# A two-block transformer step on one core: weight chunks multiplied in pairs at new buffer offsets, squares moved from POOL to ACT, first loads in another order

## The chip, the cores and the metric

The kernel runs on one core of one Trainium2 chip. The metric is the device time of one execution in microseconds (us). The profile is of one execution, and the times are medians of several runs.

## The reference, cut to what matters

256 positions with a width of 2048 pass through two transformer blocks in float32. Block 1: a banded attention (16 heads) beside a gated linear attention, an output projection, a feed-forward part with a causal convolution (5632 wide), and a gated side input, which this text calls the ple stage. Block 2: a sliding-window attention beside a stick-breaking attention, two gated branches, an output projection and a second feed-forward part. Nearly all arithmetic is in products with weight matrices that are read once:

```python
x = x + jnp.concatenate([y_a, y_g], axis=-1) @ w_out[i]
h = rms_norm(x, norm_ffn_w[i])
u = causal_depthwise_conv(h @ w_ffn_up[i], w_ffn_conv[i], b_ffn_conv[i])
u_gate, u_val = jnp.split(u, 2, axis=-1)
x = x + (jax.nn.gelu(u_gate) * u_val) @ w_ffn_down[i]
h = rms_norm(x, norm_ple_w[i])
x = x + jax.nn.sigmoid(h @ w_ple_gate[i]) * (p[i] @ w_ple_proj[i])
...
merged = jax.nn.sigmoid(ga) * ya + jax.nn.sigmoid(gb) * yb
x = x + merged @ w_out[layer]
x = x + swiglu(rmsnorm(x, norm_ffn_g[layer]), w_ffn_in[layer], w_ffn_down[layer])
```

Each norm needs the sum over the width of the squares of x.

## The kernel before

**Products.** Activations are held transposed (width on the 128 partitions, 256 positions along the row). A float32 product is made of fp32r products: each operand is the sum of a high part (its cast to fp32r, made by ACT) and a low part (the rest, made by DVE). An activation tile (`xa`, `g`, `m`, `pt`) holds high and low part side by side, 512 columns. A weight tile of 128x128 takes two matmuls: its high part against all 512 columns, its low part against the 256 high columns alone. Both accumulate in one PSUM bank, and the evacuation adds the bank's halves: ACT copies one half (`jb`, line 311), DVE adds the other (`jo`, by way of the helper in line 114).

**Chunks.** Weights come in chunks of 512 KB (128x1024: 4 tiles of the sum's index kk by 2 tiles of the output's index m, so 8 weight tiles). SP loads a chunk into one of 5 `raw` buffers; `split` (line 181) lets ACT write the high part (line 195) and DVE the low part (line 196) into one of 4 `hi` and one of 4 `lo` buffers. These are 1152 wide, and the chunk starts `off` elements into both: 48 (192 bytes), 80 for `w_out_2`, 72 for the ple stage's resident weights. `job_t` (line 236) makes one job, that is two output tiles, of several chunks, and takes two of four PSUM banks (`lin`). `overlap` (line 267) interleaves the first two jobs of a stage.

**Order.** Everything is put out in one hand-made order, and each engine runs its own part of it in that order. `run` (line 198) goes through the chunks: `open` (line 218) puts out loads and splits up to two chunks ahead (three in the ple stage), `multiply` (line 212) the matmuls, `step` (line 126) lets the generators of the evacuations, norms and attention heads each go on to their next `yield`, and `after` starts the evacuation of a job that has ended. `multiply` goes by runs of two tiles: two high matmuls, then the two low ones:

```python
for b in range(0, len(ch.tiles), RUN):        # RUN = 2
    for lo in range(2):
        for m, kk in ch.tiles[b:b + RUN]:
            ch.product(ch, m, kk, lo)
```

**The ple stage** (line 979) alternates a gate job of four chunks with one resident chunk of half the size (`pt`, 4 weight tiles), eight times. `ev_proj` (line 1009) takes the two output tiles of a resident chunk one after the other: in one step, for each, ACT's copy, DVE's sum, its product with the gate and its addition to x, then `sum_squares` (line 334): POOL squares x and POOL adds the square to `acc`. Two steps later, for each: ACT scales x, ACT and DVE make the next block's activation tile `g` from it, ACT squares it, POOL adds the square to `accb`.

**The start.** `start` (line 522) loads `mix_w` by ACT's queue, and puts out the loads of chunk 0 ahead of the rest: two halves of `x_in` and the second half of the weights on SP's queue, the first half of the weights on ACT's (`queues`). Nine matmuls of ones against ones follow, with nothing to compute.

Of the kernel before, what the change touches and what calls it, by code (L numbers as in the profile page):

```python
# [10 lines left out]
F32R = mybir.dt.float32r  # L11
# [6 lines left out]
P = 128  # L18
T = 256
D = 2048  # L20
KD = D // P
EPS = 1e-6
D_FF = 5632
KF = D_FF // P
# [26 lines left out]
RAW = 5  # L51
HL = 4
AHEAD = 2
RUN = 2

OFF = 48
OFF_OF = {"w_out_2": 80, None: 72}
LIN = 4


# [8 lines left out]
class Chunk:  # L69
# [6 lines left out]
    def __init__(self, dram, n, needs, mm, before=None, after=None, resident=None):  # L76
        self.dram, self.n, self.needs, self.mm = dram, n, needs, mm
        self.before, self.after, self.resident = before, after, resident
        self.pre_load = self.pre_split = None
        self.cuts, self.pack = 1, None  # L80
        self.ahead, self.queues = AHEAD, ()
        self.off, self.product, self.tiles = 0, None, None
        self.raw = self.hi = self.lo = None

    def of(self, part, n):
# [5 lines left out]
class Builder:  # L91
# [75 lines left out]
    def load_ahead(self, upto):  # L167

        while self.loaded < min(len(self.chunks), upto):
            ch = self.chunks[self.loaded]  # L170
            if ch.dram is not None:
                ch.raw = self.raw_p.tile([P, 1024], F32, tag="raw", name="raw")[:, :ch.n]
                for i in range(ch.cuts):
                    part = ch.of(i, ch.n)
                    if ch.pre_load:
                        ch.pre_load(i)
                    q = ch.queues[i] if i < len(ch.queues) else self.nc.sync
                    q.dma_start(ch.raw[:, part], ch.dram[:, part])
            self.loaded += 1

    def split(self, ch):
        hi = self.hl_p.tile([P, 1152], F32R, tag="hi", name="hi")[:, ch.off:]
        lo = self.hl_p.tile([P, 1152], F32R, tag="lo", name="lo")[:, ch.off:]
        ch.hi, ch.lo = hi[:, :2 * ch.n if ch.pack else ch.n], lo[:, :ch.n]
        raw = ch.resident() if ch.resident else ch.raw
        for i in range(ch.cuts):
            part = ch.of(i, ch.n)
            if ch.pre_split:
                ch.pre_split(i)
            r, hi, lo = raw[:, part], ch.hi[:, part], ch.lo[:, part]  # L190
            if ch.pack:
                r = r.rearrange("p (k c) -> p k c", c=ch.pack)
                both = ch.hi.rearrange("p (k s c) -> p k s c", s=2, c=ch.pack)
                hi, lo = both[:, :, 0], both[:, :, 1]
            self.nc.scalar.copy(hi, r)  # L195
            self.tt(lo, r, hi.bitcast(F32), ALU.subtract)

    def run(self):

        self.loaded = 0  # L200
        self.done = 0
        for i, ch in enumerate(self.chunks):
            self.open(i, ch.ahead)
            if ch.mm:
                ch.mm(ch)
            else:
                self.multiply(ch)
            self.step()
            if ch.after:
                ch.after()  # L210

    def multiply(self, ch):
        for b in range(0, len(ch.tiles), RUN):
            for lo in range(2):
                for m, kk in ch.tiles[b:b + RUN]:
                    ch.product(ch, m, kk, lo)

    def open(self, i, ahead):
# [14 lines left out]
        self.live_lin += 1  # L233
        return self.lin_p.tile([P, 512], F32, tag="lin", name="lin")

    def job_t(self, w, k0, kn, j, src, evac, before=None, resident=None, banks=None):

        ps = []
        for b in range(0, kn, 4):
            n = min(4, kn - b)

            def product(ch, m, kk, lo, b=b):
                k = b + kk
                if not ps:
                    ps.extend(banks() if banks else [self.lin_tile(), self.lin_tile()])
                at = kk * 256 + m * P
                self.nc.tensor.matmul(  # L250
                    ps[m][:, T:] if lo else ps[m], lhsT=(ch.lo if lo else ch.hi)[:, at:at + P],
                    rhs=src.tile[k][:, :T] if lo else src.tile[k], start=not lo and k == 0,
                    stop=bool(lo) and k == kn - 1, skip_group_check=True)
            after = None
            if b + n == kn:
                def after():
                    for m in range(2):
                        self.hot.append(evac(m, ps[m]))
            self.chunks.append(Chunk(
                None if resident else self.a[w][j, (k0 + b) // 4], n * 256,  # L260
                [(src, b + kk) for kk in range(n)], None, before=None if b else before,
                after=after, resident=resident))
            c = self.chunks[-1]
            c.off = OFF_OF.get(w, OFF)
            c.product, c.tiles = product, [(m, kk) for m in range(2) for kk in range(n)]

    def overlap(self, at, n):
# [204 lines left out]
    def block1(self):  # L472
        nc, a = self.nc, self.a
        h = Src(KD)
# [47 lines left out]
        def start():  # L522
            self.inv = None
            self.mix_w = s1.tile([P, KD], F32, tag="mix_w", name="mix_w")
            nc.scalar.dma_start(self.mix_w, a["mix_w"])
            self.load_ahead(1)
            nc.scalar.preload_act_table_set(LOG_SET)
            self.act_set = LOG_SET
            self.make_consts()

            ps = self.bank2(1)[:, 0, :P]
            for _ in range(9):
                nc.tensor.matmul(ps, lhsT=self.ones, rhs=self.ones, start=True, stop=True)
            self.wup = s1.tile([2 * RANK + 1, GH * DK], F32, tag="S", name="wup")
            self.lr = s1.tile([2 * RANK + 1, T], F32, tag="kt", name="lr")
            nc.gpsimd.memset(self.lr, 1.0)
# [23 lines left out]
            self.chunks[2 * i].pre_load = load_x(i)  # L560
            self.chunks[2 * i].pre_split = scale_x(i)
        self.chunks[0].cuts = 2
        self.chunks[0].queues = (nc.scalar,)
        self.chunks[0].tiles.sort(key=lambda t: t[1])
        for j in range(2):
            self.job_t("w_gq", 0, KD, j, h,
# [94 lines left out]
        for j in range(KD // 2):  # L661
            self.job_t("w_out", 0, KD, j, y,
                       self.ev_res(2 * j, h2, "norm_ffn_w", self.xa, "xa", lambda: acc2[0]),
                       before=open_x if j == 0 else None)
        self.overlap(at, 4)

    def put_y(self, y, k, x):
# [228 lines left out]
    def ffn(self, wu, wd, conv):  # L896
        nc, a = self.nc, self.a
        h = self.h_ffn
# [22 lines left out]
        for si, (f0, fn) in enumerate(segs):  # L921
            g = Src(fn)

            def ev_gate(j0):
                def ev(m, ps):
                    o = yield from conv_of(ps, j0 + m)
                    gt = self.ft.tile([P, T], F32, tag="gt", name="gt", bufs=4)
                    self.act(gt, o, AF.Gelu_apprx_tanh if conv else AF.Silu)
                    st[j0 + m] = gt
                return ev  # L930
# [9 lines left out]

            at = len(self.chunks)
            for j in range(f0, f0 + fn, 2):
                self.job_t(wu, 0, KD, j // 2, h, ev_gate(j))
                self.job_t(wu, 0, KD, (KF + j) // 2, h, ev_val(j))
            if si == 0:
                self.overlap(at, 4)
            final = si == len(segs) - 1
# [7 lines left out]
            for j in range(KD // 2):  # L955
                if not final:
                    ev = ev_down(2 * j)
                elif conv:
                    ev = self.ev_res(2 * j, out, "norm_ple_w", self.xa, "xa", lambda: acc[0])
                else:  # L960
                    ev = self.ev_final(2 * j)
                before = None
                if final and j == 0:
                    def before():
                        acc.append(self.new_acc())
                        self.acc_f = acc[0]
                        if conv:
                            self.open_ple()
                self.job_t(wd, f0, fn, j, g, ev, before=before)
            self.overlap(at, fn // 4)  # L970


# [6 lines left out]
    def ple(self):  # L979
# [29 lines left out]
        def ev_proj(k0):  # L1009
            def ev(m, ps):  # L1010
# [5 lines left out]
                gt = st.pop(k)  # L1016
                self.tt(t, t, gt, ALU.mult)
                self.tt(x, x, t, ALU.add)
                self.sum_squares(accs[0], x, k == 0)
                yield  # L1020
                yield

# [51 lines left out]
    def block2(self):  # L1074
# [123 lines left out]
            order += [("a", j), ("b", j)]  # L1198
        for kind, j in order:
            if kind == "a":  # L1200
                self.job_t("w2_ga", 0, KD, j, h, ev_ga(2 * j, ga))
                self.job_t("w_branch_a_2", 0, 8, j, ya, ev_ba(2 * j, ga))
            else:
                self.job_t("w2_gb", 0, KD, j, h, ev_ga(2 * j, gb))
                self.job_t("w_branch_b_2", 0, 8, j, yb, ev_bb(2 * j, gb),
                           before=close_att if j == 0 else None)
        h2 = Src(KD)
        self.h_ffn = h2
        acc = []
# [1 line left out]
        for j in range(KD // 2):  # L1211
            self.job_t("w_out_2", 0, KD, j, mg,
                       self.ev_res(2 * j, h2, "norm_ffn_g_2", self.xa, "xa", lambda: acc[0]),
                       before=(lambda: acc.append(self.new_acc())) if j == 0 else None)

        self.overlap(at, 4)
        self.close_mg = es2.close
# [218 lines left out]
```

## Time and profile before

| what | value |
|---|---|
| median of 3 runs | 2600.23 us (2600.16 to 2602.01) |
| profiled execution, its own time | 2600.7 us |
| its span, first to last instruction | 2599.0 us |
| mean granted TensorE clock | 0.998 |
| TensorE matmul busy | 2576.2 us, 99% of the span |
| DVE, ACT, POOL busy | 66%, 52%, 21% |

PE is TensorE's matmuls, PEld its weight loads, which run beside them. The duration of a matmul in the profile is from its start to its modelled end, and neighbours overlap; the rate is read from the starts of neighbouring matmuls. The profiled execution is 0.5 us over the median, and 1.7 us of its time lie outside the span.

### The profile page before, as it was taken

Reading aid. Unit: us, or ns where it says so; the run is one execution under the profiler, and the core shown is the slowest. Engines: PE = TensorE matmul, PEld = TensorE weight load, DVE = VectorE, ACT = ScalarE, POOL = GpSimd, SP = SyncE. Lnnn points to the kernel's source line nnn. Section 1 sums busy time; section 2 is a strip of 40 time slices with the busy share of each in tenths; the row PEclk is TensorE's granted clock in tenths of the full one; section 3 lists DMA queues with packets and bytes.
Section 4 is the critical chain, followed back from the end, with each engine's and each line's share of the span. In section 5 each row is a group of like instructions: output and inputs, shape, how many; then the busy total and the mean of one; then the engine's idle time right before and its main releaser. Section 6 shows DMA issues by size and latency. Waiting matters only on the chain.

```text
span 2599.0 us, 39038 instructions
## 1 busy us (share of the span) xinstructions
PE 2576.2 (99%) x14860; PEld 2239.3 (86%) x14860; DVE 1726.0 (66%) x2241; ACT 1351.2 (52%) x2018; POOL 556.8 (21%) x638
## 2 busy tenths in 40 slices
PE   9999999999999999999999999999999999999997
PEld 7888888888888888887878888888888888888886
DVE  7457677776677667778776766666665656555565
ACT  5545545564556445556555655554554444543543
POOL 5121232220122012346431111112311001100114
PEclk9999999999999999999999999999999999999999
DMA  7556575666666666654555456665666666666663
GB/s 245 157 163 191 168 234 186 195 190 193 187 191 190 193 187 190 223 175 149 167 152 156 148 166 199 192 189 191 189 193 189 193 191 190 192 190 190 191 192 124
DMA packets 133752, 480.36 MB, mean 185 GB/s; under 512 B 15067, under 2 KB 17371, under 8 KB 133436
## 3 DMA queue, kind: packets, MB, share of 16 engines
q1 hardware_dynamic: 131964, 474.19, 58.8%
q8 instruction: 116, 1.90, 0.3%
q0 software_dynamic: 736, 2.36, 0.3%
q10 hardware_dynamic: 864, 1.32, 0.1%
q14 instruction: 72, 0.59, 0.1%
HBM read 475.71 MB, written 2.10 MB: 184 GB/s over the span
## 4 chain that ended last, share of the span: by engine, by line
PE 93%; DVE 2%; POOL 1%; issue 1%; ACT 1%; DMA 0%; DVEq 0%; ACTq 0%; SPq 0%
PE lin L250 84%; PE lin L292 4%; PE lin L290 2%; DVE lo L114 1%; POOL cu L1002 1%; PE c L774 1%; DVE jo L114 1%; PE c L724 1%; PE c L761 0%; ACT hi L195 0%; PE c L250 0%; DMA x_in<-in_xT 0%; PE c L1253 0%; DVE x L114 0%; POOL x_in L506 0%
## 5 line engine op out<-in xcount | busy, mean ns | idle before, releaser
L114 DVE TENSOR_TENSOR lo<-raw,hi 128x1024 fp32r<-128x1024 f32 (+1 forms) x889 | 1133.2, 1286 | 616.6 <-ACT hi L195 614.2
L195 ACT CAST hi<-raw 128x1024 fp32r<-128x1024 f32 (+1 forms) x890 | 923.6, 1046 | 556.7 <-PE lin L250 501.1
L250 PE MATMUL lin<-xa,hi 128*128 128x512 f32 x3808 | 1186.6, 393 | 1.7 <-ACT hi L195 1.7
L250 PEld LDWEIGHTS lin<-xa,lo 128*128 128x128 f32 x3808 | 715.3, 188 | 162.6 <-DVE lo L114 6.2
L250 PE MATMUL lin<-g,hi 128*128 128x512 f32 x2592 | 807.4, 393 | 0.3 <-DVE jo L114 0.3
L250 PE MATMUL lin<-xa,lo 128*128 128x256 f32 x3808 | 753.7, 279 | 2.0 <-DVE lo L114 2.0
L250 PEld LDWEIGHTS lin<-xa,hi 128*128 128x128 f32 x3808 | 577.7, 188 | 4.5 <-issue 2.3
L250 PEld LDWEIGHTS lin<-g,lo 128*128 128x128 f32 x2592 | 486.7, 188 | 108.8 <-DVE lo L114 2.0
L250 PE MATMUL lin<-g,lo 128*128 128x256 f32 x2592 | 512.3, 279 | 0.8 <-DVE lo L114 0.8
L250 PEld LDWEIGHTS lin<-g,hi 128*128 128x128 f32 x2592 | 392.5, 188 | 3.7 <-issue 2.4
L910 POOL TENSOR_TENSOR cu<-jo,inv 128x256 f32<-128x256 f32 x176 | 133.2, 757 | 1083.3 <-DVE jo L114 1083.3
L311 ACT COPY jb<-lin 128x256 f32<-128x256 f32 x313 | 114.1, 372 | 193.1 <-PE lin L250 189.3
L114 DVE TENSOR_TENSOR jo<-lin,jb 128x256 f32<-128x256 f32 x297 | 122.3, 419 | 84.7 <-ACT jb L311 59.5
L329 ACT CAST g<-gt 128x256 fp32r<-128x256 f32 x88 | 35.8, 407 | 117.5 <-DVE gt L114 59.1
L117 DVE SCALAR_TENSOR_TENSOR co<-cu,vecs,co 128x255 f32<-128x255 f32 (+1 forms) x176 | 89.5, 529 | 3.1
L342 POOL TENSOR_TENSOR acc<-acc,sq 128x256 f32<-128x256 f32 x73 | 88.9, 1218 | 5.7
L340 POOL TENSOR_TENSOR sq<-x 128x256 f32<-128x256 f32 x73 | 55.2, 756 | 151.9 <-DVE x L114 151.7
L250 PE MATMUL lin<-m,hi 128*128 128x512 f32 x256 | 79.4, 392 | 0.0
L114 DVE TENSOR_TENSOR g<-gt,g 128x256 fp32r<-128x256 f32 x88 | 49.1, 558 | 25.0 <-ACT g L329 25.0
L114 POOL TENSOR_TENSOR gt<-gt,co 128x256 f32<-128x256 f32 x44 | 53.7, 1220 | 55.2 <-DVE co L117 55.2
L1155 POOL TENSOR_TENSOR u<-jo,inv 128x256 f32<-128x256 f32 x32 | 24.6, 772 | 176.9 <-DVE jo L114 176.9
L114 DVE TENSOR_TENSOR jo<-lin,x 128x256 f32<-128x256 f32 x128 | 53.1, 415 | 6.5 <-PE lin L250 6.5
(215 smaller groups left out, 1624.9 us busy)
## 6 DMA issues: line engine op xcount, KB each, us to landing
raw<-in_w_ffn_up SPq DMA_DIRECT2D x176, 512.0 KB, 4.1
raw<-in_w_ffn_down SPq DMA_DIRECT2D x176, 512.0 KB, 4.1
raw<-in_w_ffn_in SPq DMA_DIRECT2D x176, 512.0 KB, 3.8
raw<-in_w_out SPq DMA_DIRECT2D x64, 512.0 KB, 4.5
raw<-in_w_aq SPq DMA_DIRECT2D x32, 512.0 KB, 4.0
raw<-in_w_ple_gate SPq DMA_DIRECT2D x32, 512.0 KB, 4.0
raw<-in_w_ga SPq DMA_DIRECT2D x32, 512.0 KB, 3.7
raw<-in_w_gb SPq DMA_DIRECT2D x32, 512.0 KB, 3.7
```

Source lines behind the costliest of these rows:

```text
L114: (eng or self.nc.vector).tensor_tensor(out, a, b, op)
L117: self.nc.vector.scalar_tensor_tensor(out, in0=in0, scalar=scalar, in1=in1, op0=op0, op1=op1)
L195: self.nc.scalar.copy(hi, r)
L250: self.nc.tensor.matmul(ps[m][:, T:] if lo else ps[m], lhsT=(ch.lo if lo else ch.hi)[:, at:at + P], rhs=src.tile[k][:, :T] if lo else src. ...
L290: self.nc.tensor.matmul(ps[t][:, :wd], lhsT=xl, rhs=wt, start=k == 0, stop=False)
L292: self.nc.tensor.matmul(ps[t][:, :wd], lhsT=xh, rhs=wt, start=False, stop=bool(lo) and k == KD - 1)
L311: self.nc.scalar.copy(b[:n], ps[:n, T:])
L329: self.nc.scalar.copy(t[:, :T], x)
L340: g.tensor_tensor(sq, x, x, ALU.mult)
L342: g.tensor_tensor(acc, acc, sq, ALU.add)
L724: self.nc.tensor.matmul(ps[:, r, o], lhsT=q[r][rows[r], qs], rhs=k[rows[r], ks], start=True, stop=True, skip_group_check=True)
L910: nc.gpsimd.tensor_tensor(u, t, self.inv[:, :T], ALU.mult)
```

## The change

Chunks of jobs that are marked `paired` go two at a time where both have their operands: 16 high matmuls of both chunks, then their 16 low ones. Marked are `w_out`, both feed-forward parts, the branch and gate jobs of block 2 from the third pair on, and `w_out_2`: 32 + 264 + 72 + 32 + 264 = 664 chunks with 5,312 weight tiles. In them the high parts start 63 elements (252 bytes) into the buffer, the low parts 48 (192 bytes) as before; both are moved by the same 32 elements more for `w_out_2`. The others keep runs of two and their offsets. In `ev_proj`, the square for `acc` moves from POOL to ACT. Chunk 0's loads lose their place ahead of the others and their part on ACT's queue, and 11 matmuls of ones replace 9.

```diff
-RUN = 2
-OFF = 48
-OFF_OF = {"w_out_2": 80, None: 72}
+OFF = (48, 48)
+OFF_PAIRED = (63, 48)
+MORE_OFF = {"w_out_2": 32, None: 24}
...
-                    q = ch.queues[i] if i < len(ch.queues) else self.nc.sync
-                    q.dma_start(ch.raw[:, part], ch.dram[:, part])
+                    self.nc.sync.dma_start(ch.raw[:, part], ch.dram[:, part])
...
-        hi = self.hl_p.tile([P, 1152], F32R, tag="hi", name="hi")[:, ch.off:]
-        lo = self.hl_p.tile([P, 1152], F32R, tag="lo", name="lo")[:, ch.off:]
+        hi = self.hl_p.tile([P, 1152], F32R, tag="hi", name="hi")[:, ch.off[0]:]
+        lo = self.hl_p.tile([P, 1152], F32R, tag="lo", name="lo")[:, ch.off[1]:]
...
+        i = 0
+        while i < len(self.chunks):
+            some = self.chunks[i:i + 1]
+            self.open(i, some[0].ahead)
+            for ch in self.chunks[i + 1:i + 2]:
+                if (ch.paired and some[0].paired and not ch.before
+                        and all(src.ready[k] for src, k in ch.needs)):
+                    self.open(i + 1, AHEAD)
+                    some.append(ch)
+            if some[0].mm:
+                some[0].mm(some[0])
             else:
-                self.multiply(ch)
-            self.step()
-            if ch.after:
-                ch.after()
+                self.multiply([(ch, m, kk) for ch in some for m, kk in ch.tiles],
+                              16 if len(some) == 2 else 2)
+            for ch in some:
+                self.step()
+                if ch.after:
+                    ch.after()
+            i += len(some)
...
-            c.off = OFF_OF.get(w, OFF)
+            c.paired = paired
+            c.off = tuple(x + MORE_OFF.get(w, 0) for x in (OFF_PAIRED if paired else OFF))
...
-            self.load_ahead(1)
             nc.scalar.preload_act_table_set(LOG_SET)
...
-            for _ in range(9):
+            for _ in range(11):
                 nc.tensor.matmul(ps, lhsT=self.ones, rhs=self.ones, start=True, stop=True)
...
-        self.chunks[0].queues = (nc.scalar,)
...
                 self.tt(x, x, t, ALU.add)
-                self.sum_squares(accs[0], x, k == 0)
+                self.sum_squares(accs[0], x, k == 0, on_act=True)
                 yield
                 yield
```

## Rows read from the trace of the kernel before

**Rows 1.** The page's first part: engine, busy us, share of the span, instructions.

```profile
PE 2576.2 (99%) x14860; PEld 2239.3 (86%) x14860; DVE 1726.0 (66%) x2241; ACT 1351.2 (52%) x2018; POOL 556.8 (21%) x638
```

**Rows 2.** Windows, PE alone: window, length, busy (matmuls), clock, DMA share, GB/s.

```profile
420.00:1150.00 730.00, 730.00 (x4233) 1.00 0.63 193
1870.00:2480.00 610.00, 610.00 (x3538) 1.00 0.62 191
```

**Rows 3.** Timeline of PE: start, us, engine line operation, out<-in, count; feed-forward part.

```profile
2000.30 0.62 PE L250 MATMUL lin<-xa,hi 128*128 128x512 f32 x2
2000.76 0.39 PE L250 MATMUL lin<-xa,lo 128*128 128x256 f32 x2
2000.99 0.62 PE L250 MATMUL lin<-xa,hi 128*128 128x512 f32 x2
2001.44 0.40 PE L250 MATMUL lin<-xa,lo 128*128 128x256 f32 x2
2001.68 0.62 PE L250 MATMUL lin<-xa,hi 128*128 128x512 f32 x2
```

**Rows 4.** Timeline of PE: long run of 512-column matmuls, weights as moving operand.

```profile
107.25 0.39 PE L290 MATMUL lin<-hi,xa 128*128 128x512 f32 x1
...
109.06 1.07 PE L292 MATMUL lin<-lo,xa 128*128 128x512 f32 x4
```

**Rows 5.** Timeline of PE: long run of 256-column matmuls, weights as moving operand.

```profile
1258.65 0.28 PE L290 MATMUL lin<-hi,g 128*128 128x256 f32 x1
...
1260.57 1.12 PE L292 MATMUL lin<-lo,g 128*128 128x256 f32 x8
```

**Rows 6.** Timeline of PE: a resident chunk of the ple stage, one period earlier.

```profile
1203.05 0.62 PE L250 MATMUL c<-pt,hi 128*128 128x512 f32 x2
```

**Rows 7.** Timeline, all engines: one period of the ple stage; in brackets idle time and releaser.

```profile
1212.95 0.35 ACT L311 COPY jb<-c 128x256 f32<-128x256 f32 x1
...
1213.87 0.37 ACT L311 COPY jb<-c 128x256 f32<-128x256 f32 x1 [0.56 <-DVE jo L114]
...
1214.14 0.62 ACT L195 CAST hi<-w_ple 128x512 fp32r<-128x512 f32 x1
1214.33 0.42 DVE L114 TENSOR_TENSOR x<-x,jo 128x256 f32<-128x256 f32 x1
...
1214.84 0.61 POOL L340 TENSOR_TENSOR sq<-x 128x256 f32<-128x256 f32 x1 [2.24 <-DVE x L114]
...
1215.61 0.51 ACT L111 ACTIVATE x<-x,vecs 128x256 f32<-128x256 f32 x1
...
1215.76 0.86 DVE L114 TENSOR_TENSOR x<-x,jo 128x256 f32<-128x256 f32 x1
...
1216.64 0.62 PE L250 MATMUL c<-pt,hi 128*128 128x512 f32 x2
...
1217.73 0.51 ACT L111 ACTIVATE x<-x,vecs 128x256 f32<-128x256 f32 x1 [0.77 <-POOL sq L340]
...
1219.41 0.42 ACT L111 ACTIVATE sq<-x 128x256 f32<-128x256 f32 x1 [0.62 <-POOL acc L342]
...
1219.73 1.98 ACT L195 CAST hi<-raw 128x1024 fp32r<-128x1024 f32 x2
```

**Rows 8.** Timeline of the start: matmuls of ones, chunk 0's first load, cast and matmul.

```profile
1.05 4.21 PE L533 MATMUL c<-ones 128*128 128x128 f32 x18 [1.05 <-POOL ones L439]
...
1.24 0.45 ACTq L178 DMA_DIRECT2D raw<-in_w_gk  x1
...
6.28 0.62 ACT L195 CAST hi<-raw 128x512 fp32r<-128x512 f32 x1 [1.11 <-DMA raw<-in_w_gk]
...
6.95 1.22 PE L250 MATMUL lin<-xa,hi 128*128 128x512 f32 x2 [1.69 <-ACT hi L195]
```

**Rows 9.** Timeline of PE: the first norm's sum over the width.

```profile
34.56 0.67 PE L375 MATMUL c<-acc,ones 128*128 128x256 f32 x2 [0.73 <-DVE acc L114]
```

**Rows 10.** Timeline of DVE at the end: the last output tile.

```profile
2584.24 0.42 DVE L114 TENSOR_TENSOR jo<-lin,x 128x256 f32<-128x256 f32 x1 [0.51 <-PE lin L250]
```

More of the change, by code (lines that the diff above doesn't have):

```diff
@@ L80, in __init__ @@
         self.cuts, self.pack = 1, None
-        self.ahead, self.queues = AHEAD, ()
-        self.off, self.product, self.tiles = 0, None, None
+        self.ahead = AHEAD
+        self.off, self.product, self.tiles, self.paired = (0, 0), None, None, False
         self.raw = self.hi = self.lo = None
@@ L201, in run, with multiply @@
         self.done = 0
[L202 to L205, printed above, removed]
-            else:
-                self.multiply(ch)
-            self.step()
-            if ch.after:
-                ch.after()
-    def multiply(self, ch):
-        for b in range(0, len(ch.tiles), RUN):
+        i = 0
[9 more added lines that the diff above has]
+                some[0].mm(some[0])
+            else:
+                self.multiply([(ch, m, kk) for ch in some for m, kk in ch.tiles],
[5 more added lines that the diff above has]
+            i += len(some)
+    def multiply(self, tiles, run):
+        for b in range(0, len(tiles), run):
             for lo in range(2):
-                for m, kk in ch.tiles[b:b + RUN]:
+                for ch, m, kk in tiles[b:b + run]:
                     ch.product(ch, m, kk, lo)
@@ L234, in lin_tile, with job_t @@
         return self.lin_p.tile([P, 512], F32, tag="lin", name="lin")
-    def job_t(self, w, k0, kn, j, src, evac, before=None, resident=None, banks=None):
+    def job_t(self, w, k0, kn, j, src, evac, before=None, resident=None, banks=None,
+              paired=False):
         ps = []
@@ L663, in block1 @@
                        self.ev_res(2 * j, h2, "norm_ffn_w", self.xa, "xa", lambda: acc2[0]),
-                       before=open_x if j == 0 else None)
+                       before=open_x if j == 0 else None, paired=True)
         self.overlap(at, 4)
@@ L942, in ffn @@
             for j in range(f0, f0 + fn, 2):
-                self.job_t(wu, 0, KD, j // 2, h, ev_gate(j))
-                self.job_t(wu, 0, KD, (KF + j) // 2, h, ev_val(j))
+                self.job_t(wu, 0, KD, j // 2, h, ev_gate(j), paired=True)
+                self.job_t(wu, 0, KD, (KF + j) // 2, h, ev_val(j), paired=True)
             if si == 0:
@@ L968, in before @@
                             self.open_ple()
-                self.job_t(wd, f0, fn, j, g, ev, before=before)
+                self.job_t(wd, f0, fn, j, g, ev, before=before, paired=True)
             self.overlap(at, fn // 4)
@@ L1200, in block2 @@
             if kind == "a":
-                self.job_t("w2_ga", 0, KD, j, h, ev_ga(2 * j, ga))
-                self.job_t("w_branch_a_2", 0, 8, j, ya, ev_ba(2 * j, ga))
+                self.job_t("w2_ga", 0, KD, j, h, ev_ga(2 * j, ga), paired=j > 1)
+                self.job_t("w_branch_a_2", 0, 8, j, ya, ev_ba(2 * j, ga), paired=j > 1)
             else:
-                self.job_t("w2_gb", 0, KD, j, h, ev_ga(2 * j, gb))
+                self.job_t("w2_gb", 0, KD, j, h, ev_ga(2 * j, gb), paired=j > 1)
                 self.job_t("w_branch_b_2", 0, 8, j, yb, ev_bb(2 * j, gb),
-                           before=close_att if j == 0 else None)
+                           before=close_att if j == 0 else None, paired=j > 1)
         h2 = Src(KD)
@@ L1213, in block2 @@
                        self.ev_res(2 * j, h2, "norm_ffn_g_2", self.xa, "xa", lambda: acc[0]),
-                       before=(lambda: acc.append(self.new_acc())) if j == 0 else None)
+                       before=(lambda: acc.append(self.new_acc())) if j == 0 else None,
+                       paired=True)
         self.overlap(at, 4)
```

## The prediction, made before the run

> **What bounds the kernel now.** I read the page first. PE is busy for 99% of the span and no other engine for more than 66% [rows 1], so whatever does not lengthen or shorten PE's own stream costs nothing, and the stream's rate is the first question. The windows of the two feed-forward parts give it: 4,233 matmuls in 730.00 us, 3,538 in 610.00 [rows 2], that is 172.4 ns per matmul and 345 ns per weight tile (one high, one low matmul), with no idle time at the full clock. The timeline shows what the 345 ns are made of: from one group of four to the next 0.69 us, of which two high matmuls take 0.45 or 0.46 (225 to 230 ns each) and two low ones 0.23 or 0.24 (115 to 120 each) [rows 3]. The other place to read is the ple stage, where PE does wait. Its period, from one resident chunk to the next, is 1216.64 - 1203.05 = 13.59 us [rows 6, 7], while 4 gate chunks and a resident one are 36 weight tiles, or 36 x 0.345 = 12.42. So 1.17 us of each period are lost, and what sets it is the order of work on ACT and DVE: ACT casts the weights of a chunk only when PE already needs them.
>
> The sum is made against the profiled execution, 2600.7 us, which stands 0.5 over the median of the runs.
>
> **Part 1, pairs and offsets.** 664 chunks with 5,312 weight tiles change their order and the place of their high parts. No matmul is added or removed. In a pair 15 of 16 high matmuls follow a high one, and 15 of 16 low ones a low one, so a tile costs one interval in a long run of each sort. No row shows this kernel's weights in such a run, or at 252 bytes. The nearest rows are the runs with the operands exchanged: 8 matmuls of 512 columns in 109.06 - 107.25 = 1.81 us, 226 ns each [rows 4], and 16 of 256 columns in 1260.57 - 1258.65 = 1.92 us, 120 ns each [rows 5]. Against them stand this kernel's own intervals, 225 to 230 and 115 to 120. The low end is 225 + 115 = 340 ns, the high end 230 + 120 = 350; times 5,312 that is -26.6 to +26.6 us. I take 226 for the high one, as in the long run, and 119 for the low one, near the long run but a little down, because the low parts keep their offset and have been seen at 115. That is 345 ns, and a change of 0.
>
> [...]
>
> **Part 2, what a pair holds up.** A pair lasts 16 x 0.345 = 5.5 us and holds two of the four high and low buffers. The casts for the next pair can start once its predecessor's high run is over, and ACT has two of them per 5.5 us at 52% busy [rows 1]: cost 0, and if that cover failed, each late cast would show as a PE wait. Where two overlapped jobs end in one pair (10 stage heads), their banks are wanted at once. The first job's low parts end 0.92 us and more before the pair does, and its two outputs take four DVE sums of 0.42 us (the duration in [rows 10]), so I take 0; with a weight split in front of them it would be 1 us each, +10 at the most, the lower end being 0 too, as nothing is released earlier. At the very end of the kernel the first of the last two outputs is complete 4 low matmuls (0.46 us) before the last matmul, now 4 tiles (1.38). It loses 0.92; DVE idles 0.51 there today [rows 10] and takes that up: **+0.4 us**.
>
> **Part 3, squares on ACT.** This is the part that I expect to decide. Per period POOL loses two squares and ACT gains two of about 0.42 us. ACT also loses two waits for POOL, 0.77 and 0.62 [rows 7]. That looks like a gain. But ACT works in order, and the new square stands behind DVE's addition to x and ahead of the second tile's copy `jb` and of the next casts. Step by step from [rows 7]: the first copy starts at 1212.95, and x is complete at 1214.33 + 0.42 = 1214.75. ACT's square starts at 1214.84, where POOL's does now, and ends at 1215.26. Only then the second copy runs (now 1213.87); it needs the same 1.80 us to its x (1212.95 to 1214.75), so x is there at 1217.06, and the second square ends at about 1217.57. Now the cast of the resident weights starts, which stood at 1214.14: 3.4 us later. From there to the scaling of x 1.47 us stay (1214.14 to 1215.61): 1219.04. The first tile's three ACT operations take 1217.73 - 1215.61 - 0.77 = 1.35, the second's 1219.73 - 1217.73 - 0.62 = 1.38, and the next cast starts at 1221.77 instead of 1219.73: 2.0 us later per turn of the loop. ACT's next turn starts from that cast, so the loop grows by that, and PE, which already waits for it, waits 2.0 more: for the resident weights' cast about 1.5 (they are wanted at 1216.64 and would be ready at 1218.2), then the rest at the next gate chunk. There are seven whole turns between eight resident chunks: **7 x 2.0 = +14.0 us**. Low end: only the waits and the squares count, 0.84 - 1.39 = -0.55 per turn, -4.4 over eight. High end: the 3.4 us at the cast in full, +24. I take the worked-out chain.
>
> **Part 4, the start.** The first weights move to SP's queue, behind the first half of x, and each later SP load comes 0.45 us later (the duration of an issue) [rows 8]; ACT's queue loses one issue. Today the first cast waits 1.11 us for these weights, and the first matmul runs at 6.95 [rows 8]. Between 1.1 us earlier and 0.45 later; either way PE then waits 0.73 us for the first norm's sum [rows 9], which ends with the last load of x and its squares, not with PE. Cost 0; without that cover -1.1 to +0.45. Eighteen recorded matmuls of ones take 4.21 us; four more (two calls) take 0.9 and end at about 6.2, before 6.95: cost 0, hidden by the same wait for the cast.
>
> **Sum.** 0 + 0.4 + 14.0 + 0 = +14.4 us: 2615.1 for the profiled execution, **2614.6 us** as a median (2600.2 + 14.4).
>
> **Rivals.**
> - *The pairs pay more than the ple stage loses (faster).* The place is the 5,312 tiles, the price up to 5 ns each; it decides from 14.4 / 5,312 = 2.7 ns per tile on. For it: both levels are there in today's stream, and 340 ns would only make the better one permanent [rows 3]. Against it: both long runs sit near the upper level for the low ones [rows 4, 5]. At 340 ns: 2614.6 - 26.6 = 2588. Chance 0.22.
> - *The pairs cost.* Long runs lock into the upper level, or the 252 bytes hurt: at 346 ns 2620, at 350 ns 2641. For it: 120 ns in the long run [rows 5]. Chance 0.17.
> - *The squares help.* The generators' order leaves ACT other work to do, and only the waits for POOL go: -4.4 + 0.4 gives 2596. For it: the 0.77 and 0.62 us; DVE's addition to x takes 0.86 beside POOL's work against 0.42 [rows 7]. The Trainium skill (SBUF — State Buffer, section Who interferes with whom) says that a DVE instruction with two SBUF inputs contends with a GpSimd instruction that reads SBUF; the two additions agree with it. Against it: the copy, the square and the next copy come out of one generator after the other in one step. Chance 0.12.
> - *The pairs don't form* because operands are not marked ready in time: then part 1 is 0 for those chunks, and the time is the forecast's.
>
> **How the numbers follow.** The forecast, with 2602 to 2630, has 0.45, and 0.04 goes to causes not named. About 0.2% (5 us) is what a measurement of this kernel can tell from no change. Faster by more: most of the first rival (0.15), half of the third (0.06), 0.01 of the rest: 0.22. Within it: the parts of these two near the present time (0.07 and 0.06): 0.13. Slower: 0.65. The range reaches from 2592, which takes in the third rival and the upper half of the first, to 2632, which takes in the pairs' cost up to 348 ns.
>
> **What would show it.** The windows of the feed-forward parts give the tile: 345 ns if part 1 is right, 342 or less for the first rival, 347 or more for the second. In the ple stage the period between resident chunks should be near 15.6 us, ACT should wait for DVE's x ahead of each square, and PE should wait for the cast of `w_ple`. PE's wait for the first norm should be there still. I am wrong if the period stays at 13.6 or falls, or if the feed-forward windows move by more than 2.7 ns per tile.

## The result and the profile after

The changed kernel takes **2641.84 us** (median; 2640.4 to 2642.6), the kernel before beside it 2600.48: a ratio of 1.0157 [1.014, 1.0175], 41.4 us slower. Slower was forecast (2614.6), but the time lies outside the range (2592 to 2632). The profiled execution took 2641.56 us.

The page's first part, as [rows 1]:

```profile
PE 2607.0 (99%) x14864; PEld 2250.8 (85%) x14864; DVE 1678.4 (64%) x2241; ACT 1350.0 (51%) x2034; POOL 527.6 (20%) x622
```

PE is still at work all the time, with four matmuls more (of ones, at the start) and 30.8 us more of it. So the stream itself has become slower. Stage lengths, from the starts of their first matmuls in both traces:

| stage | before | after | difference |
|---|---|---|---|
| up to `w_out` | 320.2 | 319.9 | -0.3 |
| `w_out` | 100.0 | 101.1 | +1.1 |
| first feed-forward part | 729.1 | 743.2 | +14.1 |
| ple stage | 105.7 | 118.3 | +12.6 |
| block 2 to its branches' end | 511.5 | 509.6 | -1.9 |
| `w_out_2` | 99.5 | 101.2 | +1.7 |
| second feed-forward part | 718.0 | 731.1 | +13.1 |

Windows of PE in the two feed-forward parts, as [rows 2]:

```profile
420.00:1150.00 730.00, 730.00 (x4157) 1.00 0.60 190
...
1930.00:2480.00 550.00, 550.00 (x3134) 1.00 0.58 187
```

Two matmuls per weight tile: 2 x 730 / 4157 = 351.2 ns, and 351.0 in the second, where before had 345 [rows 2]. The clock is full and PE never idles. The timeline of PE there, as [rows 3]:

```profile
2000.54 3.89 PE L262 MATMUL lin<-xa,hi 128*128 128x512 f32 x16
2004.27 2.05 PE L262 MATMUL lin<-xa,lo 128*128 128x256 f32 x16
2006.15 3.89 PE L262 MATMUL lin<-xa,hi 128*128 128x512 f32 x16
```

Sixteen high matmuls take 3.73 us, 233 ns each; sixteen low ones 1.88 us, 118 each. The median intervals are these to the ns in 296 of the 332 pairs. The other 36 are those of block 2's branches. Timeline of PE where they end and `w_out_2` begins:

```profile
1786.69 3.79 PE L262 MATMUL lin<-xa,hi 128*128 128x512 f32 x16
1790.32 1.98 PE L262 MATMUL lin<-xa,lo 128*128 128x256 f32 x16
1792.14 3.90 PE L262 MATMUL lin<-m,hi 128*128 128x512 f32 x16
1795.88 2.05 PE L262 MATMUL lin<-m,lo 128*128 128x256 f32 x16
1797.77 3.89 PE L262 MATMUL lin<-m,hi 128*128 128x512 f32 x16
```

At the offsets of the feed-forward parts, the branch pairs run at 3.63 / 16 = 227 and 1.82 / 16 = 113 ns, 340 per tile, and from the first `m` on (weights 128 bytes further) it is 351. Below, the two are called the slow and the fast stream.

The ple stage: timeline of PE (first two lines: turns of the loop, as the 1216.64 of [rows 7]) and three waits that were shorter or not there before (none, 1.23 and 0.21 us). The first of the three stands at the norm ahead of the stage and is part of the +14.1:

```profile
1238.36 0.74 PE L262 MATMUL c<-pt,hi 128*128 128x512 f32 x2 [1.12 <-ACT hi L195]
...
1253.25 0.73 PE L262 MATMUL c<-pt,hi 128*128 128x512 f32 x2 [1.15 <-ACT hi L195]
```

```profile
1164.21 0.70 PE L388 MATMUL c<-acc,ones 128*128 128x256 f32 x2 [0.77 <-POOL acc L355]
...
1193.66 1.02 PE L262 MATMUL c<-pt,hi 128*128 128x512 f32 x2 [3.13 <-ACT hi L195]
...
1282.50 0.46 PE L303 MATMUL lin<-hi,g 128*128 128x256 f32 x1 [3.36 <-ACT hi L195]
```

A turn takes 14.89 us instead of 13.59. ACT's timeline shows why:

```profile
1248.29 0.36 ACT L324 COPY jb<-c 128x256 f32<-128x256 f32 x1
1250.12 0.42 ACT L112 ACTIVATE sq<-x 128x256 f32<-128x256 f32 x1 [1.48 <-DVE x L115]
1250.45 0.35 ACT L324 COPY jb<-c 128x256 f32<-128x256 f32 x1
1252.28 0.42 ACT L112 ACTIVATE sq<-x 128x256 f32<-128x256 f32 x1 [1.48 <-DVE x L115]
1252.60 0.60 ACT L195 CAST hi<-w_ple 128x512 fp32r<-128x512 f32 x1
```

Before each square ACT stands idle for 1.48 us until DVE has x. From the first copy to the cast of the resident weights it now takes 4.31 us, in [rows 7] 1.19.

The start, as [rows 8, 9]:

```profile
5.77 0.86 PE L262 MATMUL lin<-xa,hi 128*128 128x512 f32 x2
...
34.24 0.67 PE L388 MATMUL c<-acc,ones 128*128 128x256 f32 x2 [0.78 <-DVE acc L115]
```

The first matmul runs 1.2 us earlier; the wait for the first norm is there as before (0.78 and 0.73 us), and 0.3 us are left of it.

### The profile page after: what moved, and what is told of

The parts are those of the page before. It is cut to its first block, busy times and chain, and to the rows that moved or that the text cites. A ratio compares the mean times of both kernels' runs of the same rounds, so it can differ in the third digit from the quotient of the medians.

```text
span 2639.6 us, 39353 instructions
## 1 busy us (share of the span) xinstructions
PE 2607.0 (99%) x14864; PEld 2250.8 (85%) x14864; DVE 1678.4 (64%) x2241; ACT 1350.0 (51%) x2034; POOL 527.6 (20%) x622
## 4 chain that ended last, share of the span: by engine, by line
PE 93%; DVE 2%; ACT 2%; POOL 1%; issue 1%; DMA 0%; DVEq 0%; SPq 0%; ACTq 0%
PE lin L262 84%; PE lin L305 4%; PE lin L303 2%; ACT hi L195 1%; PE c L785 1%; DVE jo L115 1%; PE c L735 1%; POOL cu L1013 1%; DVE x L115 0%; PE c L262 0%; PE c L772 0%; DVE lo L115 0%; PE c L1265 0%; ACT sq L112 0%; DMA raw<-in_w_gk 0%
## 5 line engine op out<-in xcount | busy, mean ns | idle before, releaser
L115 DVE TENSOR_TENSOR lo<-raw,hi 128x1024 fp32r<-128x1024 f32 (+1 forms) x889 | 1099.7, 1271 | 676.2 <-issue 349.2
L262 PE MATMUL lin<-xa,hi 128*128 128x512 f32 x3808 | 982.9, 395 | 0.6 <-DVE xa L118 0.4
L262 PEld LDWEIGHTS lin<-xa,hi 128*128 128x128 f32 x3808 | 673.9, 188 | 121.3 <-issue 2.3
L262 PE MATMUL lin<-g,hi 128*128 128x512 f32 x2592 | 667.6, 394 | 0.3 <-DVE jo L115 0.3
L262 PEld LDWEIGHTS lin<-xa,lo 128*128 128x128 f32 x3808 | 530.7, 188 | 55.9 <-DVE lo L115 5.6
L262 PE MATMUL lin<-xa,lo 128*128 128x256 f32 x3808 | 544.1, 280 | 2.2 <-DVE lo L115 2.2
L262 PEld LDWEIGHTS lin<-g,hi 128*128 128x128 f32 x2592 | 458.1, 188 | 82.5 <-issue 2.4
L262 PEld LDWEIGHTS lin<-g,lo 128*128 128x128 f32 x2592 | 360.4, 188 | 35.0 <-DVE lo L115 0.7
L262 PE MATMUL lin<-g,lo 128*128 128x256 f32 x2592 | 368.5, 279 | 0.3 <-DVE lo L115 0.3
L112 ACT ACTIVATE co<-cu,vecs 128x256 f32<-128x256 f32 x88 | 52.9, 603 | 101.5 <-POOL cu L921 97.4
L115 DVE TENSOR_TENSOR jo<-lin,x 128x256 f32<-128x256 f32 x128 | 53.2, 416 | 30.9 <-PE lin L262 30.8
```

The costliest lines, as they stand in the source:

```text
L112: self.nc.scalar.activation(out, in_, func, **kw)
L115: (eng or self.nc.vector).tensor_tensor(out, a, b, op)
L262: self.nc.tensor.matmul(ps[m][:, T:] if lo else ps[m], lhsT=(ch.lo if lo else ch.hi)[:, at:at + P], rhs=src.tile[k][:, :T] if lo else src. ...
```

## The experiments

**Order or place, pairs or squares?** The first four runs take one part each: the changed kernel with runs of two in its pairs; with the high parts back at 192 bytes; the kernel before with the square on ACT alone; the changed kernel with both parts at 0 bytes.

```diff
# e1_run2
-                              16 if len(some) == 2 else 2)
+                              2)
# e2_off48
-OFF_PAIRED = (63, 48)
+OFF_PAIRED = (48, 48)
# e3_squares, on the kernel before
-                self.sum_squares(accs[0], x, k == 0)
+                self.sum_squares(accs[0], x, k == 0, on_act=True)
# e4_off0
-OFF_PAIRED = (63, 48)
+OFF_PAIRED = (0, 0)
```

> The changed kernel with pairs kept, high parts at 252 bytes, but runs of two again (two high, two low). Theory A (the long run of one sort costs the 6.2 ns per weight tile): feed-forward windows back at 345 ns per tile, time near 2641.8 - 33 = 2609. Theory B (the 252 bytes cost it): 351 ns stay, time near 2642. Theory C (both are needed): between, 347 to 349, some 2625.

> The changed kernel with runs of 16, but high and low parts of paired chunks both at 192 bytes. Theory A (long run): 351 ns per tile stay, 2642. Theory B (offset): 345 or less, near 2609. Theory C: between.

> The kernel before with the squares for acc on ACT and nothing else. My chain: the ple stage's loop grows by 1.3 to 2.0 us per turn, the stage by 10 to 14, the time is 2611 to 2615. The rival (only the waits for POOL go): 2596. A third view, that the stage was longer in the changed kernel because of the pairs ahead of it: 2600.

> The changed kernel with runs of 16 and both parts of paired chunks at the buffer's start (0 bytes), where the exchanged-operand runs of the kernel before stood at 226 and 120 ns. If those rows carry over: 346.7 ns per tile, near 2618. If the long run costs at any offset (theory A): 351 or more, 2642 or more. If offsets matter in steps of the address: any value, and the first two runs tell less than they seem to.

The kernel before took 2601.49 us beside them. e1: 2643.17, e2: 2614.33, e3: 2614.91, e4: 2632.09. These four, and e5 to e8, e10 to e14 and e17, are single runs; kernels that ran more often spread over 1 to 3 us. So the order of the run does nothing to the rate, the place of the high parts is the loss in the stream, and the square on ACT costs 13.4 us by itself: 12.5 in the ple stage, which is 118.2 us long, and 0.9 in block 2. The window of PE in e2's first feed-forward part, and its timeline:

```profile
425.00:1130.00 705.00, 705.00 (x4091) 1.00 0.59 194
```

```profile
2001.55 3.84 PE L262 MATMUL lin<-xa,hi 128*128 128x512 f32 x16
2005.23 1.98 PE L262 MATMUL lin<-xa,lo 128*128 128x256 f32 x16
2007.04 3.82 PE L262 MATMUL lin<-xa,hi 128*128 128x512 f32 x16
2010.70 2.05 PE L262 MATMUL lin<-xa,lo 128*128 128x256 f32 x16
```

That is 344.7 ns per tile, as before; the low runs take 1.81 and 1.88 us by turns, so quicker and slower pairs alternate (5.49 and 5.54 us).

**Which places are slow?** Six further offsets in the changed kernel, with the square back on POOL. In the table below, the changed kernel, e2 and e4 have it on ACT, which costs their time some 13 us but not their rates.

```diff
-OFF_PAIRED = (63, 48)
+OFF_PAIRED = (0, 48)     # e5; e6 (60, 48), e7 (49, 48), e10 (62, 48), e11 (48, 49), e12 (60, 60)
...
-                self.sum_squares(accs[0], x, k == 0, on_act=True)
+                self.sum_squares(accs[0], x, k == 0)
```

> The changed kernel with its squares back on POOL, runs of 16, high parts at 0 bytes and low parts at 192. If high and low parts take their intervals each from their own offset (high 226.7 ns as in the run with both at 0, low 113 to 118 as in the run with both at 192): 341 to 345 ns per tile in the feed-forward windows, 2580 to 2601. If what counts is that both parts have the same offset: above 345, over 2605.

> As the last, but high parts at 240 bytes, a whole number of 16-byte steps, 12 bytes short of the change's 252. Theory M (252 is costly because it is no whole number of 16-byte steps): 345 ns per tile or near it, 2596 to 2606. Theory D (what counts is the distance from the activation operand, and 252 is simply in a bad stretch): near 351 ns, 2628 to 2635.

> As the last, but high parts at 196 bytes, one word off the good 192. Theory M (no whole number of 16-byte steps costs): near 351 ns per tile, 2628 to 2635. Theory D (distance in a smooth stretch): near 345, 2596 to 2606.

> The changed kernel with squares on POOL, runs of 16, high parts at 248 bytes (a multiple of 8, not of 16), low parts at 192. Theory M (steps of 16 bytes decide): high intervals near 233 ns, 349 to 351 per tile, 2620 to 2635. If steps of 8 bytes are enough: high intervals 226 to 230, 344 to 346 per tile, 2596 to 2606.

> The same with high parts at the good 192 bytes and low parts at 196. Theory M for weights of either sort: low intervals rise by about as much as the high ones did (4 to 6 ns over 113 to 118), 349 to 352 per tile, 2620 to 2640. If it is only beside 512 columns that an odd place costs: 345 to 346, 2600 to 2606.

> The same with high and low parts both at 240 bytes, a multiple of 16. Theory M: 344 to 347 per tile, 2595 to 2612; the low intervals tell whether 113 or 118 ns go with the offset (113 in all runs, or 118 in all) or come and go within one kernel, as they did with both at 192.

The kernel before took 2600.2 to 2600.3 us beside them. The time per tile is twice the window by its matmuls (705 us from 425, 550 us from 1930); the intervals, high and low, are means from the start of a matmul to the next, from 425 to 1130 us.

| run | bytes, high and low | us | ns per tile, first and second part | high, low |
|---|---|---|---|---|
| after | 252, 192 | 2641.84 | 351.2, 351.0 | 233, 118 |
| e2 | 192, 192 | 2614.33 | 344.7, 345.2 | 229, 116 |
| e4 | 0, 0 | 2632.09 | 347.5, 348.0 | 228, 120 |
| e5 | 0, 192 | 2620.73 | 347.8, 348.3 | 231, 118 |
| e6 | 240, 192 | 2604.05 | 345.0, 345.6 | 227, 118 |
| e7 | 196, 192 | 2619.01 | 350.4, 345.3 | 233, 118 |
| e10 | 248, 192 | 2613.41 | 347.0, 346.9 | 233, 114 |
| e11 | 192, 196 | 2618.23 | 347.6, 347.6 | 229, 118 |
| e12 | 240, 240 | 2611.53 | 345.2, 348.1 | 228, 117 |

None of these is clearly under 345. High parts at multiples of 16 bytes (0, 192, 240) run at 227 to 231 ns, those at 196, 248 and 252 at 233; this fits a step of 16 bytes, but the changed kernel's own 36 fast pairs, 227 at 252 bytes, speak against the address alone. e7 shows the same: 350.4 in one stage and 345.3 in another at the same offsets, the low interval being 118 in one and 113 in the other.

**Squares without the wait, and the start.** The square stays on ACT, but two steps later, when x has long been there: in the kernel before (e8), and in the changed kernel with pairs never formed and the offsets of before (e9). The edit in e9; in e8 the line that goes has no `on_act`:

```diff
                 self.tt(x, x, t, ALU.add)
-                self.sum_squares(accs[0], x, k == 0, on_act=True)
                 yield
                 yield
+                self.sum_squares(accs[0], x, k == 0, on_act=True)
```

> The kernel before with the square for acc on ACT, but put out two steps later, just ahead of the scaling of x, so that it stands behind no DVE work and blocks no copy. My chain: the loop loses the waits for POOL (1.39 us) and gains two squares (0.8): 0 to 0.6 us less per turn, time 2596 to 2601. If ACT's mere load of squares cost the 13 us of the third run, and not their place: 2608 to 2615 again.

> The version that should beat both: the changed kernel with no pairs and all offsets at 192 bytes as before, its first loads, and the square for acc on ACT two steps later (as in the eighth run). If the two parts add up: 2596.2 from the late squares and 0 to 1.2 us less from the first loads, 2595 to 2596; if the first norm's sum hides the start, 2596.

e8 took 2596.18 us beside 2600.19, e9 2596.48 beside 2600.31 (ratio 0.9985 [0.9976, 0.9994]): both faster than before, and no different with the changed start. ACT's timeline in e8:

```profile
1210.48 0.36 ACT L311 COPY jb<-c 128x256 f32<-128x256 f32 x1
1211.39 0.38 ACT L311 COPY jb<-c 128x256 f32<-128x256 f32 x1 [0.56 <-DVE jo L114]
1211.66 0.62 ACT L195 CAST hi<-w_ple 128x512 fp32r<-128x512 f32 x1
1212.18 1.05 ACT L195 CAST hi<-raw 128x1024 fp32r<-128x1024 f32 x1
1213.13 0.42 ACT L111 ACTIVATE sq<-x 128x256 f32<-128x256 f32 x1
```

The same square waits for nothing here, and the cast comes 1.18 us after the first copy. A turn takes 13.11 to 13.16 us, the stage 102.0: 3.7 us less than before, where the square behind DVE's sum cost 12.6.

**Two speeds at one address.** The base is now the changed kernel with the late squares. e13 puts one lone matmul of ones ahead of every fourth pair, of 8 to 128 columns (its result is not used). e14 lays `m` so that it starts as `xa` and `g` do. e15 keeps pairs in the branch stage alone.

```diff
# e13_kicks
+    def kick(self):                    # called ahead of each pair
+        self.pairs += 1
+        if self.pairs % 4 == 3:
+            n = KICKS[self.pairs // 4 % len(KICKS)]
+            ps = self.bank2(0)[:, 0, :n]
+            self.nc.tensor.matmul(ps, lhsT=self.ones_r, rhs=self.suf[:, :n], start=True, stop=True)
# e14_m_even
-MORE_OFF = {"w_out_2": 32, None: 24}
+MORE_OFF = {None: 24}
...
+            self.mgp.tile([P, 96], F32, tag="pad", name="pad")
# e15_branch_pairs: paired=True taken from w_out, w_out_2 and both feed-forward parts
```

> The changed kernel with the accumulator squares on ScalarE two steps later, and ahead of every fourth pair one lone matmul of ones (columns 128, 64, 32, 16, 8, 112, 96 and so on, to the other accumulator bank), about 83 of them. Theory S (the two speeds at the same addresses are states that a disturbance of the matmul stream can flip and that then last): after some of the lone matmuls the pairs of the up and down projections run at 227 and 113 ns instead of 233 and 118, and some pairs of the branch stage lose that; time anywhere between 2602 and 2630. Theory P (the fast state belongs to something else in the branch stage, such as what the other engines or the DMAs do there): every pair outside the branch stage stays at 351 ns per tile and every one inside at 340, time 2624 to 2640.

> The changed kernel with the accumulator squares on ScalarE two steps later, and the merged operand tiles of the second output projection laid 384 bytes further, so that they start as the other operands do (64 bytes past a multiple of 512), with the same offset for their weights as elsewhere. Theory S (a state that a disturbance flips; here the step of 128 bytes of the moving operand at the first pair of this projection): the fast pairs of the branch stage go on at 340 ns per tile through the second output projection and the second FFN, 148 pairs less by 16 x 10.8 ns = 0.17 us each, 25 us in all, so 2599. Theory P (the fast state belongs to the branch stage itself): the slow state returns at the first pair of the projection, 2624.

> Pairs at 252 and 192 bytes in the branch stage alone (36 pairs, the ones that ran at 340 ns per tile), everything else unpaired at 192 bytes as before, accumulator squares on ScalarE two steps later, the changed first loads. If the speed of the branch pairs is kept: 2596.5 less 576 tiles x 4.6 ns = 2.6 us, so 2594. If the state falls otherwise: 576 tiles x 6.2 ns = 3.6 us more, 2600.

e13 took 2626.64 us, e14 2622.23, e15 2594.14 (ratio 0.9977 [0.9967, 0.9986]). PE's timeline in e13, around a lone matmul of 80 columns and the next one, of 72:

```profile
487.44 2.06 PE L273 MATMUL lin<-xa,lo 128*128 128x256 f32 x16
489.33 0.20 PE L231 MATMUL c<-suf,ones_r 128*128 128x80 f32 x1
489.36 3.87 PE L273 MATMUL lin<-xa,hi 128*128 128x512 f32 x16
493.07 1.98 PE L273 MATMUL lin<-xa,lo 128*128 128x256 f32 x16
494.89 3.80 PE L273 MATMUL lin<-xa,hi 128*128 128x512 f32 x16
...
509.41 1.98 PE L273 MATMUL lin<-xa,lo 128*128 128x256 f32 x16
511.23 0.20 PE L231 MATMUL c<-suf,ones_r 128*128 128x72 f32 x1
511.26 3.96 PE L273 MATMUL lin<-xa,hi 128*128 128x512 f32 x16
515.06 2.05 PE L273 MATMUL lin<-xa,lo 128*128 128x256 f32 x16
516.95 3.42 PE L273 MATMUL lin<-xa,hi 128*128 128x512 f32 x14
```

The low run takes 1.89 us ahead of the first (slow), 1.82 in the four pairs after it (fast), and 1.89 again after the second. Each of the ten lone matmuls of 80 or 112 columns, all in a slow stream, turned it fast, and all ten of 72 or 96, all in a fast one, turned it slow. Up to 64 columns none made a slow stream fast for more than its first high run. Of the other lengths, 68 made it fast in three cases of four, 100 made it slow in the three cases where it was fast, and 120 and 128 left it slow each time. So the speed is a state of the stream, which a disturbance changes and which then lasts. But 80 and 112 met only the slow stream, 72 and 96 only the fast stream: a rival, that each of these four turns whichever state it meets, is not excluded, and what the length itself does stays open.

In e14 the fast stream outlives the start of `w_out_2` and ends at the next norm. PE's timeline:

```profile
1872.46 1.98 PE L262 MATMUL lin<-xa,lo 128*128 128x256 f32 x16
1874.28 0.59 PE L388 MATMUL c<-acc,ones 128*128 128x256 f32 x2
1874.52 4.08 PE L262 MATMUL lin<-xa,hi 128*128 128x512 f32 x16
1878.43 2.05 PE L262 MATMUL lin<-xa,lo 128*128 128x256 f32 x16
```

So in the changed kernel it was the other start of `m` or its weights' offset (e14 changes both) that ended the fast stream; with that mended, the norm's two matmuls end it. e14's gain was 18 pairs instead of the 148 expected.

**Three lone matmuls.** If the state lasts, a lone matmul behind each known disturbance is enough. e16 is e14 with three of 80 columns; e17 is e16 with the high parts at 192 bytes; e18 has the first of the three behind a wait that had ended the state in e16.

```diff
-        if self.pairs % 4 == 3:
+        if self.pairs in (3, 21, 205):       # e18: (6, 21, 205)
...
+            ps = self.bank2(0)[:, 0, :80]
# e17_three_192
-OFF_PAIRED = (63, 48)
+OFF_PAIRED = (48, 48)
```

> The kernel of e14_m_even with three lone matmuls of ones, 80 columns each, ahead of pairs 3, 21 and 205: one in the first output projection, one two pairs after the norm sums of each FFN. Theory S: each flips the stream from 233 and 118 ns to 227 and 113 ns, and the state lasts to the next disturbance, so 272 pairs gain 16 x 10.7 ns = 0.171 us each, 46.6 us in all: 2622.2 - 46.6 = 2575.6, faster than the kernel before by 1.0%. Rival: the fast state does not last over a hundred pairs, or the norm sums in the first FFN leave another state, so that the third matmul or the second turns fast pairs slow: between 2592 (one FFN lost) and 2622 (nothing gained).

> The kernel of e16_three with the high parts of the pairs back at 192 bytes, as the low ones. If the lone matmuls alone hold the fast state: 227 and 113 ns after them as at 252 bytes, 2577. If 252 bytes are needed for a state that lasts, the pairs alternate as in e2_off48, 345 ns per tile, and the time is that of e9_late_start, 2596.

> The kernel of e16_three with its first lone matmul ahead of pair 6 in place of pair 3, that is behind the wait of 0.57 us for a low part that ended the fast state there at pair 5. If any disturbance of the stream (a wait too) resets the state and a lone matmul of 80 columns turns it fast: the 13 pairs from 6 to 18 gain and two lose, 11 x 0.171 = 1.9 us, so 2575.4. If the first fall had another cause, it stays at 2577.

e16 took 2577.31 us, e18 2576.28 (ratios 0.9907 [0.9891, 0.9924] and 0.9906 [0.9889, 0.9924]), e17 2596.22. Both e16 and e18 beat both kernels clear of the noise: 23 to 24 us under before and 65 under the changed one, of which the late squares have a part. The three lone matmuls alone are worth 45 (e16 against e14). PE's timeline in e16, first at the wait and then at the second lone matmul:

```profile
340.18 1.98 PE L271 MATMUL lin<-g,lo 128*128 128x256 f32 x16
342.72 3.96 PE L271 MATMUL lin<-g,hi 128*128 128x512 f32 x16 [0.57 <-DVE x L116]
346.52 2.05 PE L271 MATMUL lin<-g,lo 128*128 128x256 f32 x16
...
433.15 0.20 PE L229 MATMUL c<-suf,ones_r 128*128 128x80 f32 x1
433.19 3.87 PE L271 MATMUL lin<-xa,hi 128*128 128x512 f32 x16
436.90 1.98 PE L271 MATMUL lin<-xa,lo 128*128 128x256 f32 x16
```

and its windows of PE:

```profile
440.00:1130.00 690.00, 690.00 (x4057) 1.00 0.62 196
...
1870.00:2550.00 680.00, 680.00 (x3998) 1.00 0.59 192
```

340.2 ns per tile in both. Behind the second lone matmul all 128 pairs up to the ple stage are fast, and so are the 54 behind block 2's unpaired work, up to the next norm; behind the third, the remaining 128 are. In e18 the 13 pairs between the wait and the first norm are fast as well (349 to 420 us), but the 1 us between e18 and e16 is within the spread of their runs (2574.5 to 2577.6). In e17 the pairs alternate as in e2, at 344.7 ns (690 us, 4,004 matmuls): at 192 bytes the lone matmuls hold nothing. So there is no such gain at 192 bytes, and at 252 the state decides whether the pairs gain or lose; no other place was tried with lone matmuls.

## Why the prediction was wrong

- **What bounds the kernel: right.** PE is at 99% in both kernels, and the change shows in its rate and in the one stage where it waits.
- **Part 1, pairs and offsets: the step that failed.** "That is 345 ns, and a change of 0": measured 351 in 296 pairs and 340 in 36. That is 4,736 x 6.2 - 576 x 5 = +26.5 us, as much as the whole miss (2641.6 against 2615.1 for the profiled execution); the small misses of the other parts nearly cancel. The bounds of 340 and 350 ns were the right two numbers, but I read them as the ends of an unknown between which a mean is likeliest. At 252 bytes they are two states, high and low interval going together (not so at 248, where e10 has 233 with 114), and a long stage sits in one of them. The 345 of before, at 192 bytes, is a mean too, but of a narrow alternation: its groups of four take 0.687 and 0.693 us by turns (343 and 347 ns per tile), as e2's pairs take 5.49 and 5.54 (343 and 346). Taking 226 and 119 from two different long runs joined intervals that the pairs at 252 bytes don't show together. The rival "the pairs cost", 2641 at 350 ns, is what happened, at a chance of 0.17; the rival "the pairs pay", 340 ns, is what the same code does in the other state (e16). Since a stage sits in one state or the other, the range should have reached both ends. Of the 41 us by which the change is slower, only the 12.6 of part 3 came for the forecast's reason.
- **A stated interval:** the Trainium skill (TensorE: Matmul & The Clock Gate, section Back-to-back issue gap) gives N/2.4 + 2.5 ns, 216 and 109 ns, as the gap of an isolated matmul, and 131 ns for 512 columns in a stream of weight loads and matmuls; neither goes by the place of the weights. The traces disagree with both, with 227 to 233 and 113 to 120 ns by place and by what ran before; the measurement decides.
- **Part 2, what a pair holds up: nearly right.** PE has no wait from 425 to 1150 us, and the tail took 0.3 us more (forecast +0.4). But the norm ahead of the ple stage now waits 0.77 us for POOL's sum (1164.21), where before had no wait; e1, with runs of two, has none either.
- **Part 3, squares on ACT: right in kind and nearly in size.** +14.0 forecast, +12.6 measured in the changed kernel, +13.4 in e3. The chain went as written: square behind DVE's x, second copy behind the square, cast behind both. Two terms were off and nearly cancel. A turn grew by 1.30 us and not 2.0: the cast of the resident weights moved by 4.31 - 1.19 = 3.12 and not 3.4, since successive operations of ACT start 0.33 us apart here where I took 0.42, the triples behind it ran faster (1.26 and 1.25) than the 1.35 and 1.38 I took, and 0.2 us more were gained up to the next copy. And it was not seven turns of one size: the seven intervals between resident chunks were 4.18, 12.46, 14.80 and four of 13.59, and became 4.20, 16.40 and five of 14.90, +9.3 in all; the remaining 3.3 is nearly all the wait of 3.36 us ahead of block 2 (0.21 before). Nor did I have a term for the clock, which fell to 0.50 behind each of the waits of 3.13 and 3.36 us (last section). The rival "the squares help" needed what e8 does, a square that waits for nothing.
- **Part 4, the start: right.** The first matmul came 1.2 us earlier, the wait for the first norm took it up, and e9 against e8 shows no gain.

## What to carry to other kernels

Where a trace shows two rates for the same instruction, ask whether they are two states before taking a mean: a stage that locks into one of them moves the time by far more than the mean suggests, with a sign that the trace of before does not show. Test such a layout with a small disturbance of the stream at the head of each stage (here one matmul of 80 columns) before it is kept or dropped. And an operation moved to an in-order engine costs what stands behind its wait, not its own duration: the same square was worth +13 us behind DVE's sum and -4 us two steps later.

## What was not expected of the hardware

- The time of a 128x128 weight tile in an unbroken stream depends on where its high part starts in SBUF (192 or 252 bytes into a buffer: 345 or 351 ns) and, at 252 bytes, on a state that lasts for over a hundred pairs: 340 or 351 ns at identical addresses (e16 and e14). A lone matmul, the two matmuls of a norm, a moving operand and weights that start elsewhere, or a wait of 0.57 us was followed by a change of it. What in the engine or the memory holds the state is open; no trace here shows it. At the other places, address and state are not told apart.
- After PE's wait of 3.13 us at 1193.66 the granted clock of the changed kernel fell, and again after that of 3.36 us at 1282.50. Windows of PE:

```profile
1190.00:1193.00 3.00, 0.53 (x4) 1.00 0.13 52
...
1194.60:1197.30 2.70, 2.70 (x9) 0.50 0.19 27
1197.60:1200.00 2.40, 2.40 (x16) 1.00 0.47 160
...
1283.00:1286.00 3.00, 3.00 (x16) 0.50 0.40 87
```

0.50 is the lower of its two levels (1.2 GHz), for some 3 us each time; nine matmuls ran in the first such window of 2.70 us, sixteen in the 2.40 us at the full clock behind it. The waits of 1.1 us in the turns between had no such effect.
